# A two-layer diffusion backbone on one core: chunk rows two ahead, standing conv tiles, two-pass projections, another pace of modulation rows

## The chip, the core and the metric

The kernel runs on one core of a Trainium2 chip. A core has five engines, each with its own in-order queue: TensorE (PE in the profile, with its weight loads as PEld) for matmuls, VectorE (DVE), ScalarE (ACT) and GpSimd (POOL) for elementwise work, and SyncE (SP), which issues the DMAs here. [...] The metric is the device time of one execution in microseconds; the median over runs is compared.

## What is computed

Two post-norm layers over 512 latent tokens and 256 context tokens, width 1024, all in float32. Layer 0 mixes tokens by gated linear attention (GLA) with a low-rank decay, layer 1 by a bidirectional state-space scan (SSD). Each is followed by a squared-ReLU MLP of width 4096 (FFN), and each sub-layer is modulated by shift, scale and gate rows made from the conditioning vectors.

```python
m_l = jnp.split((s_lat @ ada_w[i] + ada_b[i])[:, None, :], 6, axis=-1)
ul = snake(modulate(hl, m_l[0], m_l[1]))
yc, yl = gla_mixer(...)  if kind == 0  else  ssd_mixer(...)
hl = layer_norm(ALPHA * hl + m_l[2] * snake(yl), ...)
hl = layer_norm(ALPHA * hl + m_l[5] * sq_relu_mlp(modulate(hl, m_l[3], m_l[4]), w1, w2), ...)
# GLA, the low-rank part: a is 2 x 16 columns of h @ w_in
logit = einsum('blzr,zrd->zbld', a.reshape(b, l, 2, 16), w_a2) + b_a2
# SSD: 32 heads of 64 in 8 groups, state 128
z, xbc, dt = jnp.split(h @ w_in, ...)
xbc = silu(dwconv(xbc, conv_w, conv_b))          # width 5
dt = softplus(dt + dt_bias)                       # 2 directions x 32 heads
# in a chunk: y = (c . b) * exp(cum_i - cum_j, masked) @ (x * dt), plus the carried state
```

## The kernel before

Activations lie with features on the 128 partitions and tokens along the row: 512 latent and 256 context columns. To keep float32 accuracy with fast matmuls, every operand is split into a high part and a low remainder (`xh`, `xl`; `wh`, `wl`; `rh`, `rl`), and `prod` (L240) runs three terms for each block of 128 features: high by high, low activations by high weights, high activations by low weights. So a 1024-wide projection of one 128-row output is 24 matmuls for each segment of columns. A weight tile is loaded into one of four `raw` buffers (L227), cast on ScalarE (`wh`, L203) and its remainder taken on VectorE (`wl`, L204); three of each are held.

The program is written as generators. The main line issues projections; `worked` counts the columns given to TensorE, in units of 768, and after each unit may advance a `side` generator (work of the previous stage) and, every `pace[0]` units, the `background` generator `ada_rows`. One step of the latter loads a 128x1024 block of modulation weights into a `raw` buffer and makes one or two multiply-and-sum passes over it on VectorE (L157). `mod(layer, m)` drains the background until the row it needs is there. The pace is 9 at first, 12 from the GLA layer on, and 21 in FFN 0, whose first block (`bi == 0`) begins with a pre-pass of `npre` units and ends with the gate row `mod(layer, 5)`. In the FFN, ScalarE makes `rr` and `rh`, GpSimd the square `rq` (L385) and VectorE the rest `rl` (L387).

The order in which the instructions stand in each engine's queue is not that of the program text: a scheduler lays them out ahead of time, and hands out the buffers of each ring (a tag with `bufs=n`) as it goes. A load into a ring buffer is issued when the last reader of the tile that held it has been scheduled.

GLA: `first_step` (L1143) runs four projections step by step while the layer's first modulation rows come in. The third of them (`j == 2`) is the low-rank one: the weights of 32 columns are repeated three times across the 96 output rows (`wsplit(..., 32, 3)`), so that rows 0 to 31, 32 to 63 and 64 to 95 of the result are the same; the last third is replaced by its remainder, so that `aT` holds high, high and low, against `a2`, which has `gla_a2` laid out to match.

SSD: first the step projection `dt` (64 columns of weights, `prod` with three terms), `dT`, six transposes (L802), softplus, cumulative sums by matmuls with triangles (`tri`, L821), and the rows `crow` and `crowc` written to DRAM, from where they are read back broadcast over partitions. Then eight groups g0 to g7, each with four convolutions `conv`: projection, copy into a padded tile `pre` (L857, L860), whose pad columns GpSimd clears each time (L855, L856, L859), five taps on VectorE in `cv` (L867), SiLU into `cf` (L869, L870). The rest of a group is the side generator `inner(g)`, which runs while the next group's projections go on: `heads_rows` (`ec`), `natural` (TensorE transposes L877 and ScalarE copies L878 into `Bn` and `xnat`), weighted x (`xw`, L931) and states (L943), `cbs` (the products of C and B, copied at L965), then for each of four chunks the decay masks.

A chunk's rows are two tiles of the ring `L` (`LB = 7` buffers), one per direction: a DMA broadcast from `crowc` (L910), a triangular select on GpSimd (L912), four exponentials on ScalarE with a per-head bias (L998, `decays`), their sum on GpSimd (L1001, `masks`), which frees the second tile, the product with `cbs` on VectorE, and the matmuls `outputs` (L1009), which free the first. The program asks for chunk 0's rows just before the inter-chunk part and for chunk c + 1's at the end of step c:

```python
Rs, Ms = {0: chunk_rows(0)}, {}
...
    if c + 1 < NLC:
        Rs[c + 1] = chunk_rows(c + 1)
```

## Time and profile before

| | us |
|---|---|
| runs | 1951.9, 1965.13, 1965.4 |
| median | 1965.13 |
| span of the profiled execution | 1959.6 |
| TensorE busy in it | 1881.3 |
| VectorE, ScalarE, GpSimd busy | 1254.9, 798.6, 410.8 |

Stages in the trace, by when TensorE works on them: GLA projections from 10 us, FFN 0 about 440 to 960, step projection and first SSD group to 1047, the groups g0 to g7 with their inner parts to about 1500, then the SSD output projection and FFN 1 to the end. In the lists of the profile a row reads: line, engine, operation, output tile <- input tiles, shape; in brackets the time that the engine stood idle before it and what ended the idle time. In the chain of waits each row is a piece of the path that ended last: start, length, what ran. A row of stretches gives length, then busy time of TensorE, weight loads, VectorE, ScalarE and GpSimd with their counts, the granted TensorE clock, the DMA share and GB/s.

### The profile page before, as it was taken

Reading aid. Unit: us, or ns where it says so; the run is one execution under the profiler, and the core shown is the slowest. Engines: PE = TensorE matmul, PEld = TensorE weight load, DVE = VectorE, ACT = ScalarE, POOL = GpSimd, SP = SyncE. Lnnn points to the kernel's source line nnn. Section 1 sums busy time; section 2 is a strip of 40 time slices with the busy share of each in tenths; the row PEclk is TensorE's granted clock in tenths of the full one; section 3 lists DMA queues with packets and bytes.
Section 4 is the critical chain, followed back from the end, with each engine's and each line's share of the span. In section 5 each row is a group of like instructions: output and inputs, shape, how many; then the busy total and the mean of one; then the engine's idle time right before and its main releaser. Section 6 shows DMA issues by size and latency. Waiting matters only on the chain.

```text
span 1959.6 us, 29026 instructions
## 1 busy us (share of the span) xinstructions
PE 1881.3 (96%) x11405; PEld 1604.9 (82%) x11405; DVE 1254.9 (64%) x1929; ACT 798.6 (41%) x1386; POOL 410.8 (21%) x448
## 2 busy tenths in 40 slices
PE   7999999999999999999999999999999999999997
PEld 5988888788788888888897787777877788888886
DVE  4798887888655444324578888777887673333345
ACT  3445456454113123122366555455543353323231
POOL 2134242202002002010104432333321321102012
PEclk9999999999999999999999999999999999999999
DMA  8423313214444444313134433333434523333331
GB/s 329 156 73 114 104 36 106 65 55 150 141 142 140 138 137 135 116 41 116 33 107 121 129 115 112 104 101 129 121 100 132 164 73 105 96 99 96 96 89 54
DMA packets 78936, 219.01 MB, mean 112 GB/s; under 512 B 11056, under 2 KB 15792, under 8 KB 78800
## 3 DMA queue, kind: packets, MB, share of 16 engines
q1 hardware_dynamic: 78800, 217.17, 35.1%
q8 instruction: 89, 1.46, 0.3%
q14 instruction: 47, 0.39, 0.1%
HBM read 209.01 MB, written 8.13 MB: 111 GB/s over the span
## 4 chain that ended last, share of the span: by engine, by line
PE 63%; DVE 13%; DMA 7%; ACT 6%; POOL 5%; issue 5%; SPq 0%; DVEq 0%; POOLq 0%; ACTq 0%
PE mm L240 54%; DMA L<-crowc 4%; POOL L L1001 1%; ACT L L998 1%; DMA raw<-in_ada_wr_dram 1%; DVE A L593 1%; PE sm L943 1%; DVE raw L157 1%; DVE cv L867 1%; POOL L L912 1%; PE sm L676 1%; DVE wl L204 1%; POOL W L612 1%; PE sm L986 1%; PE mm L520 1%
## 5 line engine op out<-in xcount | busy, mean ns | idle before, releaser
L240 PE MATMUL mm<-xh,wh 128*128 128x512 f32 (+1 forms) x1824 | 554.2, 357 | 2.8 <-ACT xh L1044 2.6
L240 PE MATMUL mm<-xl,wh 128*128 128x512 f32 (+1 forms) x1824 | 550.0, 354 | 1.5 <-DVE xl L1045 1.5
L240 PE MATMUL mm<-xh,wl 128*128 128x512 f32 (+1 forms) x1824 | 549.7, 353 | 1.4 <-DVE wl L204 1.4
L203 ACT CAST wh<-raw 128x1024 fp32r<-128x1024 f32 (+3 forms) x227 | 227.8, 1004 | 658.5 <-PE mm L240 617.3
L204 DVE TENSOR_TENSOR wl<-raw,wh 128x1024 fp32r<-128x1024 f32 (+3 forms) x227 | 275.6, 1215 | 173.6 <-ACT wh L203 170.1
L240 PEld LDWEIGHTS mm<-xh,wh 128*128 128x128 f32 x1824 | 304.4, 189 | 54.4 <-ACT xh L1044 3.8
L240 PEld LDWEIGHTS mm<-xl,wh 128*128 128x128 f32 x1824 | 303.7, 189 | 50.6 <-issue 3.1
L240 PEld LDWEIGHTS mm<-xh,wl 128*128 128x128 f32 x1824 | 303.5, 189 | 50.7 <-DVE wl L204 2.5
L385 POOL TENSOR_TENSOR rq<-rr 128x768 f32<-128x768 f32 (+1 forms) x62 | 104.6, 1687 | 684.7 <-ACT rr L384 648.4
L240 PE MATMUL mm<-rl,wh 128*128 128x512 f32 x704 | 212.5, 355 | 3.8 <-DVE rl L387 3.8
L240 PE MATMUL mm<-rh,wl 128*128 128x512 f32 x704 | 212.4, 355 | 0.0
L240 PE MATMUL mm<-rh,wh 128*128 128x512 f32 x704 | 212.1, 355 | 0.0
L419 DVE SCALAR_TENSOR_TENSOR acc<-mm,row,acc 128x256 f32<-128x256 f32 (+1 forms) x182 | 100.7, 580 | 150.4 <-PE mm L240 150.0
L157 DVE SCALAR_TENSOR_TENSOR raw<-raw,srow 128x1024 f32<-128x1024 f32 x104 | 131.6, 1268 | 83.0 <-DMA raw<-in_ada_wr_dram 81.8
L867 DVE SCALAR_TENSOR_TENSOR cv<-pre,cvec,cv 128x770 f32<-128x770 f32 (+1 forms) x128 | 135.2, 1057 | 14.9 <-ACT cv L865 11.9
L240 PEld LDWEIGHTS mm<-rl,wh 128*128 128x128 f32 x704 | 116.0, 189 | 23.8 <-DVE rl L387 4.2
L240 PEld LDWEIGHTS mm<-rh,wh 128*128 128x128 f32 x704 | 116.1, 189 | 19.6
L240 PEld LDWEIGHTS mm<-rh,wl 128*128 128x128 f32 x704 | 116.1, 189 | 19.6
L998 ACT ACTIVATE L<-L,lcol 128x128 f32<-128x128 f32 x256 | 81.9, 393 | 69.1 <-POOL L L912 69.1
L387 DVE TENSOR_TENSOR rl<-rq,rh 128x768 fp32r<-128x768 f32 (+2 forms) x67 | 53.2, 794 | 64.0 <-POOL rq L385 63.7
L912 POOL TENSOR_SCALAR_AFFINE_SELECT L<-L 128x512 f32<-128x512 f32 x64 | 52.2, 817 | 142.5 <-DMA L<-crowc 141.4
L869 ACT ACTIVATE cf<-cv 128x512 f32<-128x512 f32 (+1 forms) x56 | 27.6, 533 | 86.5 <-DVE cv L867 86.5
(290 smaller groups left out, 2513.0 us busy)
## 6 DMA issues: line engine op xcount, KB each, us to landing
raw<-in_ffn_w_dram SPq DMA_DIRECT2D x112, 512.0 KB, 3.8
raw<-in_ada_wr_dram SPq DMA_DIRECT2D x80, 512.0 KB, 3.7
raw<-in_ssd_w_in_dram SPq DMA_DIRECT2D x48, 512.0 KB, 3.9
L<-crowc SPq DMA_DIRECT2D x64, 256.0 KB, 3.8
raw<-in_ada_w_dram SPq DMA_DIRECT2D x16, 512.0 KB, 9.1
raw<-in_gla_w_in_dram SPq DMA_DIRECT2D x16, 512.0 KB, 3.7
ec<-crow SPq DMA_DIRECT2D x64, 128.0 KB, 3.0
acc<-in_xT_dram SPq DMA_DIRECT2D x14, 384.0 KB, 6.9
```

What stands on the lines that cost most here:

```text
L157: nc.vector.scalar_tensor_tensor(o, raw, 1.0, srow[s], ALU.mult, ALU.mult, accum_out=t[:, b, s:s + 1])
L203: nc.scalar.copy(h, src)
L204: nc.vector.tensor_sub(l, src, h.bitcast(F32))
L240: nc.tensor.matmul(part_of(ps, t0, n), a[:, k, :], b[:, t0:t0 + n], start=(k == 0 and i == 0), stop=(k == kt - 1 and i == 2))
L385: eng.tensor_mul(q[:, a:b], r[:, a:b], r[:, a:b])
L387: nc.vector.tensor_sub(rl[:, a:b], q[:, a:b], rh[:, a:b].bitcast(F32))
L419: nc.vector.scalar_tensor_tensor(acc[m][:, t0:t0 + n], part_of(ps, t0, n), gate[:, m, s:s + 1], (src or acc)[m][:, t0:t0 + n], ALU.mult, A ...
L520: nc.tensor.matmul(ps[:, 256 * tt:256 * tt + 256], a, b, start=(k == 0 and i == 0), stop=(k == KT - 1 and i == 2))
L867: nc.vector.scalar_tensor_tensor(c[:, 0:n], pre[:, t:t + n], cw(t), c[:, 0:n], ALU.mult, ALU.add)
L869: nc.scalar.activation(f[:, t0:t1], c[:, t0 + d:t1 + d], AF.Tanh)
L912: nc.gpsimd.affine_select(out=L[z], in_=L[z], compare_op=ALU.is_ge, fill=NEG, base=0, pattern=[[0, 4], [1 - 2 * z, P]], channel_multiplier ...
L998: nc.scalar.activation(t[:, h, :], t[:, h, :], AF.Exp, bias=lcol[:, c, r:r + 1])
```

## The change

Five things change; comment lines go as well, so that lines below move by up to 30.

```diff
-LB = 7
+LB = 10
@@ split products
+    def wstack(src, n):
+        ts = [wpool.tile([P, KT, P], F32R, tag=t, name=nm(t), bufs=3) for t in ("wh", "wl")]
+        r = P // n
+        for t in ts:
+            v = t[:, :, 0:P - n].rearrange("p k (r n) -> p k r n", n=n)
+            nc.scalar.copy(v, src.unsqueeze(2).to_broadcast([P, KT, r - 1, n]))
+        nc.vector.tensor_sub(ts[0][:, :, P - n:], src, ts[0][:, :, 0:n].bitcast(F32))
+        nc.gpsimd.memset(ts[1][:, :, P - n:].bitcast(F32), 0.0)
+        return ts
@@ ffn, bi == 0
                     f1(m, restsegs, held[m])
+                pace[0] = 11
...
                 gate = mod(layer, 5)
+                pace[0] = 22
@@ gla_layer
-        aT = gp.tile([96, NT], F32R, tag="aT", name="aT")
+        aT = gp.tile([P, NT], F32R, tag="aT", name="aT")
...
-        for r in range(0, 96, 32):
+        for r in range(0, P, 32):
@@ ssd_layer, step projection
-            w = wsplit(wload(ssd_w_dt), KT, 64)
+            w = wpool.tile([P, KT, P], F32R, tag="wh", name="wdt", bufs=3)
+            src = wload(ssd_w_dt)
+            split_to(w[:, :, 0:64], w[:, :, 64:], src)
+            def prod_dt(segs):
+                for k in range(KT):
+                    for i in range(2):
+                        for (t0, n, _) in segs:
+                            nc.tensor.matmul(part_of(ps, t0, n), w[:, k, :], xs[k][i][:, t0:t0 + n],
+                                             start=k + i == 0, stop=k + i == KT)
+                            worked(n)
-            prod(ps, w, xs, CTXL0, KT)
+            prod_dt(CTXL0)
...
-            nc.vector.tensor_tensor(v, pt, rowb[:, 0:64].unsqueeze(1).to_broadcast(sh), ALU.add)
+            for c0, c1 in ((0, 4), (4, 6)):
+                pt = sm_ps([P, 4, P])
+                for c in range(c0, c1):
+                    nc.tensor.transpose(pt[:, c - c0, :], dT[:, c * P:(c + 1) * P], ident)
+                vc, n = v[:, c0:c1], c1 - c0
+                nc.vector.tensor_tensor(vc, pt[:, 0:n, 0:64], rowb[...], ALU.add)
+                nc.vector.tensor_add(vc, vc, pt[:, 0:n, 64:])
@@ ssd_layer, conv
+        pres = [sp.tile([P, NT + 6], F32, tag="pre", name=nm("pre"), bufs=2) for _ in range(2)]
+        for t in pres:
+            for c in (0, 514, 772):
+                nc.gpsimd.memset(t[:, c:c + 2], 0.0)
...
-            pre = sp.tile([P, NT + 6], F32, tag="pre", name=nm("pre"), bufs=2)
+            pre = pres[0]
+            pres.reverse()
-            nc.gpsimd.memset(pre[:, 0:2], 0.0)
-            nc.gpsimd.memset(pre[:, 514:516], 0.0)
-                nc.gpsimd.memset(pre[:, 772:774], 0.0)
@@ inner
             Es = [heads_rows(i) for i in range(2)]
+            Rs, Ms = {c: chunk_rows(c) for c in range(2)}, {}
...
-            Rs, Ms = {0: chunk_rows(0)}, {}
...
-                if c + 1 < NLC:
-                    Rs[c + 1] = chunk_rows(c + 1)
+                if c + 2 < NLC:
+                    Rs[c + 2] = chunk_rows(c + 2)
@@ first_step
-                for i, (a, b) in enumerate(((w[0], xs[k][0]), (w[1], xs[k][0]), (w[0], xs[k][1]))):
+                terms = ((w[0], xs[k][0]), (w[1], xs[k][0]), (w[0], xs[k][1])) if j != 2 else zip(w, xs[k])
+                for i, (a, b) in enumerate(terms):
...
-                    ws.extend((wsplit(wload(gla_w_a), KT, 32, 3),
+                    ws.extend((wstack(wload(gla_w_a), 32),
@@ program
-    nc = _bacc.Bacc("TRN2", target_bir_lowering=False, num_devices=1)
+    nc = _bacc.Bacc("TRN2", target_bir_lowering=False, num_devices=1, dynamic_dma_scratch_size=1024)
```

The low-rank projection now has high, high, high, low weights in one tile and high, high, high, zero in the other: the first multiplies the high activations, the second the low ones, and the fourth block of 32 rows carries the high-by-low term into `aT` of 128 rows, to be summed by the product with `a2`. The step projection has high and low weights side by side in one 128-column tile, and the two halves are added after the transposes. The smaller scratch of the last line gives the room for the three more `L` buffers. The matmuls of TensorE go from 10436 to 10396: 16 fewer in `first_step`, 24 fewer in the step projection. GpSimd has 85 rows fewer.

How the rows stand on ScalarE at the end of g4's projections, where it copies the transposed tiles (L878), before:

```order
L203 CAST wh_12304<-raw_12302 128x1024
L878 COPY Bn_12069<-sm_12071 128x512
L878 COPY Bn_12069<-sm_12077 128x256
L878 COPY xnat_12070<-sm_12083 128x4x128
L878 COPY xnat_12070<-sm_12089 128x2x128
L998 ACTIVATE L_12904<-L_12904,lcol 128x128 x4
L878 COPY xnat_12070<-sm_12107 128x4x128
L878 COPY xnat_12070<-sm_12113 128x2x128
L998 ACTIVATE L_12957<-L_12957,lcol 128x128 x4
L965 COPY cbs_12167<-sm_12162 128x512
```

and after the change (L907 is L878 of before, L1028 is L998, L995 is L965):

```order
L203 CAST wh_12203<-raw_12201 128x1024
L907 COPY Bn_11985<-sm_11987 128x512
L907 COPY Bn_11985<-sm_11993 128x256
L907 COPY xnat_11986<-sm_11999 128x4x128
L907 COPY xnat_11986<-sm_12005 128x2x128
L1028 ACTIVATE L_13078<-L_13078,lcol 128x128 x4
L907 COPY xnat_11986<-sm_12023 128x4x128
L907 COPY xnat_11986<-sm_12029 128x2x128
L1028 ACTIVATE L_13087<-L_13087,lcol 128x128 x4
L995 COPY cbs_12083<-sm_12078 128x512
```

Nothing moved: two rows of exponentials stand among and behind the copies in both, on a tile further on in the count. The same holds for g2, g3 and g5.

The same place in g6, before:

```order
L203 CAST wh_13446<-raw_13444 128x1024
L878 COPY Bn_13211<-sm_13213 128x512
L878 COPY Bn_13211<-sm_13219 128x256
L878 COPY xnat_13212<-sm_13225 128x4x128
L878 COPY xnat_13212<-sm_13231 128x2x128
L998 ACTIVATE L_14084<-L_14084,lcol 128x128 x4
L878 COPY xnat_13212<-sm_13249 128x4x128
L878 COPY xnat_13212<-sm_13255 128x2x128
L998 ACTIVATE L_14136<-L_14136,lcol 128x128 x4
L965 COPY cbs_13309<-sm_13304 128x512
```

and after:

```order
L203 CAST wh_13315<-raw_13313 128x1024
L919 ACTIVATE zs_13013<-mm_13020 128x512
L907 COPY Bn_13097<-sm_13099 128x512
L907 COPY Bn_13097<-sm_13105 128x256
L907 COPY xnat_13098<-sm_13111 128x4x128
L907 COPY xnat_13098<-sm_13117 128x2x128
L907 COPY xnat_13098<-sm_13135 128x4x128
L907 COPY xnat_13098<-sm_13141 128x2x128
L995 COPY cbs_13195<-sm_13190 128x512
```

The two rows of exponentials are gone from it. Between the `cbs` copies of g5 and g6 there are 32 exponentials before and 20 after, between those of g6 and g7 twelve and none, and between those of g0 and g1 40 and 64. Of the latter, 26 stand in one row right behind `cbs` of g0, ahead of `cf` of the next convolution; the last two tiles among them are each loaded when the sum (L1031) of the pair before has freed a buffer. On SP, eight loads of `L` stand behind the `ec` rows of g0 ahead of the next weight load, where two stood.

VectorE's rows in the first block of FFN 0, from the first `rl` on, before (`junk` and `raw` are the two passes of a row step):

```order
L387 TENSOR_TENSOR rl_4682<-rq_4684,rh_4681 128x768
L204 TENSOR_TENSOR wl_4796<-raw_4793,wh_4795 128x1024
L387 TENSOR_TENSOR rl_4715<-rq_4717,rh_4714 128x768
L157 SCALAR_TENSOR_TENSOR raw_4819,row_4603<-raw_4819,srow_4598 128x1024
L387 TENSOR_TENSOR rl_4785<-rq_4787,rh_4784 128x768
L204 TENSOR_TENSOR wl_4866<-raw_4863,wh_4865 128x1024
L157 SCALAR_TENSOR_TENSOR junk_4885,row_4603<-raw_4883,srow_4597 128x1024
L204 TENSOR_TENSOR wl_4936<-raw_4933,wh_4935 128x1024
```

and after (L397 is L387 of before):

```order
L397 TENSOR_TENSOR rl_4668<-rq_4670,rh_4667 128x768
L157 SCALAR_TENSOR_TENSOR raw_4752,row_4589<-raw_4752,srow_4584 128x1024
L397 TENSOR_TENSOR rl_4701<-rq_4703,rh_4700 128x768
L204 TENSOR_TENSOR wl_4787<-raw_4784,wh_4786 128x1024
L397 TENSOR_TENSOR rl_4776<-rq_4778,rh_4775 128x768
L157 SCALAR_TENSOR_TENSOR junk_4798,row_4589<-raw_4796,srow_4583 128x1024
L157 SCALAR_TENSOR_TENSOR junk_4825,row_4589<-raw_4823,srow_4583 128x1024
L157 SCALAR_TENSOR_TENSOR raw_4796,row_4589<-raw_4796,srow_4584 128x1024
L157 SCALAR_TENSOR_TENSOR raw_4823,row_4589<-raw_4823,srow_4584 128x1024
L157 SCALAR_TENSOR_TENSOR junk_4852,row_4589<-raw_4850,srow_4583 128x1024
L204 TENSOR_TENSOR wl_4867<-raw_4864,wh_4866 128x1024
```

The first `wl` moved behind the second `rl`, and five passes stand between the third `rl` and the second `wl`, where none stood. Up to the last `rl` of this block there are 84 passes since the start, 75 before.

More of the change, by code (lines that the diff above doesn't have):

```diff
@@ L494, in gla_layer @@
             ps = part_of(first[2], t0, n)
-            nc.scalar.copy(aT[:, ts], ps[0:96])
+            nc.scalar.copy(aT[:, ts], ps)
             nc.vector.tensor_sub(aT[64:96, ts], ps[64:96], aT[64:96, ts].bitcast(F32))
@@ L794, in ssd_layer @@
                 nc.sync.dma_start(accd[k], acc0[k][:, :NL])
-            prod(ps, w, xs, L1, KT)
+            prod_dt(L1)
             prod(held[1], held[0], xs, L1, KT)
-            dT = tt([64, NT], "dT")
+            dT = tt([P, NT], "dT")
             for (t0, n, _) in BOTH:
-                nc.vector.tensor_copy(dT[:, t0:t0 + n], part_of(ps, t0, n)[0:64, :])
-            pt = sm_ps([P, NCH, 64])
-            for c in range(NCH):
-                nc.tensor.transpose(pt[:, c, :], dT[:, c * P:(c + 1) * P], ident[0:64, 0:64])
+                nc.vector.tensor_copy(dT[:, t0:t0 + n], part_of(ps, t0, n))
             sh = [P, NCH, 64]
@@ L1140, in first_step @@
                 w = ws[j]
[L1141 removed]
+                terms = ((w[0], xs[k][0]), (w[1], xs[k][0]), (w[0], xs[k][1])) if j != 2 else zip(w, xs[k])
+                for i, (a, b) in enumerate(terms):
                     for (t0, n, _) in segs:
                         nc.tensor.matmul(part_of(first[j], t0, n), a[:, k, :], b[:, t0:t0 + n],
[L1144 removed]
+                                         start=(k == 0 and i == 0), stop=(k == KT - 1 and i == (1 if j == 2 else 2)))
         m = ct([P, 2, 8, 2], "ada01")
```

6 lines of the change are left out of this document (3 added, 3 removed).

## The prediction

> **What bounds the kernel.** I read the page first, then the list of what TensorE waited for, then the timelines around the longest of those waits and the chain of waits there.
>
> ```profile
> span 1959.6 us, 29026 instructions
> PE 1881.3 (96%) x11405; PEld 1604.9 (82%) x11405; DVE 1254.9 (64%) x1929; ACT 798.6 (41%) x1386; POOL 410.8 (21%) x448
> ...
> PE sm L943 <- DVE xw L931: 15.4, 9, 3.6
> PE sm L877 <- ACT Bn L878: 7.5, 4, 2.9
> PE sm L125 <- DMA raw<-in_ada_w_dram: 5.7, 2, 5.2
> ...
> PE mm L240 <- DVE rl L387: 3.8, 1, 3.8
> ...
> PE sm L877 <- DVE cf L870: 3.3, 1, 3.3
> ```
>
> TensorE is busy for 1881.3 of 1959.6 us; only 78.3 us are idle. So there are two ways to gain: fewer matmuls, or fewer of these waits. The first two rows of the waits (15.4 + 7.5 = 22.9 us) are all in the SSD layer, once or twice in each of its eight head groups g0 to g7, where the transposed B and x tiles (`Bn`, `xnat`, L878) and the weighted x (`xw`, L931) come late. The row of 3.8 us is in the first FFN. A changed wait in any other place is worth little.
>
> All sums are against the profiled execution's 1959.6 us. The median of the runs shown is 1965.13 us, 5.5 us above that span, and the runs lie between 1951.9 and 1965.4; I subtract the sum from the median.
>
> **Low-rank projection of the GLA layer in two passes.** Eight k-steps lose one term of a 512-column and a 256-column matmul: 16 matmuls. Their cadence, from the timeline of TensorE (an "x2" row is two matmuls):
>
> ```profile
> 27.68 0.51 PE L1143 MATMUL mm<-xh,wl 128*128 128x512 f32 x2
> 28.03 0.53 PE L1143 MATMUL mm<-xl,wh 128*128 128x512 f32 x2
> 28.39 0.51 PE L1143 MATMUL mm<-xh,wh 128*128 128x512 f32 x2
> ...
> 25.00:59.00 34.00, 34.00 (x294) 27.28 (x293) 21.43 (x39) 12.89 (x22) 9.10 (x17) 1.00 0.69 258
> ```
>
> The rows start 0.35 us apart, one 512 and one 256 together. The window from 25 to 59 us (the columns behind the length are TensorE, weight load, VectorE, ScalarE, GpSimd) has TensorE busy throughout, so what is removed there counts in full: 8 x 0.35 = **-2.8 us**. Against it stand a wider cast on ScalarE ahead of the first use, two more `a2` loads on SP and 128 instead of 96 rows in the `aT` copies, which cost nothing more, since rows lie side by side. The cast is no larger than a weight cast (1.0 us below). I take 0 for these with 0 to +1 us as ends, since that stage waits for the `in_ada_w` loads at its start (5.7 us above) and not for ScalarE afterwards.
>
> **Step projection of the SSD layer in two passes.** It loses 24 matmuls of 256 columns, at the cadence of this stage:
>
> ```profile
> 1005.55 0.28 PE L240 MATMUL mm<-xl,wh 128*128 128x256 f32 x1
> 1005.67 0.28 PE L240 MATMUL mm<-xh,wl 128*128 128x256 f32 x1
> 1005.79 0.28 PE L240 MATMUL mm<-xh,wh 128*128 128x256 f32 x1
> ...
> 1013.52 0.89 PE L821 MATMUL sm<-dv,tri 128*128 128x192 f32 x4 [0.88 <-DVE dv L816]
> ```
>
> 24 x 0.12 = **-2.9 us**. The chain behind it gets longer: six transposes into two tiles instead of one, and four adds on VectorE instead of one. It already ends last once: TensorE waits 0.88 us for `dv`. In the changed order more matmuls stand ahead of that row. Ends 0 and +2 us (three more adds, each below the 0.5 to 1.0 us that VectorE's rows of 512 to 770 columns show); I take **+0.5 us**, near the lower end, as work was moved in.
>
> **Chunk rows two ahead, ten buffers.** This is the part whose size is open. The last long stall of the SSD layer, in g6, read backwards in the chain of waits:
>
> ```profile
> 1415.46 1.32 POOL L L1001
> ...
> 1416.80 4.50 DMA L<-crowc
> ...
> 1421.43 0.65 POOL L L912
> ...
> 1422.10 1.28 ACT L L998 x4
> 1423.37 0.74 ACT xnat L878 x2
> ...
> 1424.14 1.26 DVE xw L931 x2
> ...
> 1425.54 1.95 PE sm L943 x4
> ...
> 1416.96 0.85 ACT L878 COPY xnat<-sm 128x512 f32<-128x512 f32 x2
> ```
>
> The mask add (L1001) frees a buffer of the ring `L`; the next load of chunk rows takes 4.50 us, its select 0.65; four exponentials (L998) of that same tile stand on ScalarE between the two pairs of `xnat` copies, so these copies, `xw` and TensorE wait for the load, although they do not need it. More buffers would cure that only if the exponentials behind a just-freed buffer moved away from the copies. The order shown with the change says they do not: from g2 to g5 ScalarE, GpSimd and SP have the same rows in the same places, with tiles three further on, and each load still waits for the mask add just ahead of it. The scheduler had run the loads ahead until the ring was full, and it does so again with a ring of ten. So I cost the stalls of g1 to g5 at no change. In g6 the loads have run out three tiles earlier: no exponentials stand among the copies, and g6's wait goes: **-3.6 us** (the longest in the first row of waits). What is late next there is `xw` itself: the first pair of copies ran at 1416.96 (last row, from ScalarE's timeline), so without the load the second pair ends at about 1418.5 and `xw` at 1419.8, before TensorE stopped (1425.5 - 3.6 = 1421.9). I count the full 3.6; ends 0 and -3.6.
>
> The 24 exponentials (six tiles of four) that leave g6 and g7, twelve from each, now stand between the `cbs` copies of g0 and g1, at 0.32 us each 7.7 us of ScalarE:
>
> ```profile
> 1066.32 0.58 ACT L965 COPY cbs<-sm 128x512 f32<-128x512 f32 x1 [3.15 <-PE sm L963]
> 1068.09 1.28 ACT L998 ACTIVATE L<-L,lcol 128x128 f32<-128x128 f32 x4 [1.19 <-POOL L L912]
> 1072.44 1.06 ACT L203 CAST wh<-raw 128x1024 fp32r<-128x1024 f32 x1 [3.08 <-PE mm L240]
> ...
> 1078.02 0.94 ACT L869 ACTIVATE cf<-cv 128x512 f32<-128x512 f32 x2 [1.28 <-DVE cv L867]
> ...
> 1085.07 1.03 ACT L203 CAST wh<-raw 128x1024 fp32r<-128x1024 f32 x1
> ...
> 1090.00:1150.00 60.00, 55.83 (x317) 45.25 (x316) 53.61 (x76) 34.30 (x74) 22.10 (x28) 1.00 0.40 123
> ```
>
> ScalarE is busy 34.3 of 60 us there, so it has room on the whole. But behind `cbs` of g0 some 25 exponentials now stand in a row ahead of `cf` (L869), and their last two tiles go round the loop of the chain above twice: 2 x (1.32 + 4.50 + 0.65 + 1.28) = 15.5 us after 1067, so `cf` comes at about 1083 instead of 1078. The next weight cast and the next `pre` copy stand behind it, and came at 1085 anyway: the lateness is taken up before TensorE sees it. I take 0. Ends: +6 us (the 5 us reach TensorE, and 1 more at the next conv) and -3 us (the stall of 3.3 us at g0 for `cf`, which fewer GpSimd rows could shorten). On SP eight L loads instead of two stand ahead of a weight load, 6 x 0.33 us of issue; that weight's cast comes over 15 us later.
>
> ```profile
> L910 SPq DMA_DIRECT2D L<-crowc x64: 319/326/1569, 1023.6 to 1457.5; - x64
> 1390.87 0.10 POOL L855 MEMSET pre<- 128x2 f32 x1 [6.66 <-DVE cv L867]
> ```
>
> **Standing conv tiles.** Some 85 memsets of 0.10 us or less go from GpSimd, which is 21% busy. In the chain above GpSimd waits for a DMA, not for a memset: 0, ends -2 and 0 us.
>
> **Pace of the modulation rows.** It matters in the first block of FFN 0 alone. There VectorE makes `wl` (L204) and `rl` (L387) for TensorE, and a row step is two passes (L157) of 1.15 us each from start to start (the first two rows):
>
> ```profile
> 455.12 1.21 DVE L157 SCALAR_TENSOR_TENSOR junk<-raw,srow 128x1024 f32<-128x1024 f32 x1
> ...
> 456.27 1.21 DVE L157 SCALAR_TENSOR_TENSOR raw<-raw,srow 128x1024 f32<-128x1024 f32 x1
> ...
> 458.85 0.96 DVE L387 TENSOR_TENSOR rl<-rq,rh 128x768 fp32r<-128x768 f32 x1 [1.35 <-POOL rq L385]
> 459.72 1.22 DVE L204 TENSOR_TENSOR wl<-raw,wh 128x1024 fp32r<-128x1024 f32 x1
> 462.30 0.96 DVE L387 TENSOR_TENSOR rl<-rq,rh 128x768 fp32r<-128x768 f32 x1 [1.36 <-POOL rq L385]
> ...
> 465.75 0.96 DVE L387 TENSOR_TENSOR rl<-rq,rh 128x768 fp32r<-128x768 f32 x1 [1.35 <-POOL rq L385]
> ...
> 510.34 1.22 DVE L157 SCALAR_TENSOR_TENSOR junk<-raw,srow 128x1024 f32<-128x1024 f32 x1 [3.70 <-DMA raw<-in_ada_wr_dram]
> ...
> 513.63 1.01 PE L240 MATMUL mm<-rl,wh 128*128 128x512 f32 x2 [3.83 <-DVE rl L387]
> ```
>
> The wait of 3.83 us is there because the rows are late at the end of the block: VectorE stands in a row step whose load has not landed (3.70 us) ahead of `rl`. With 11 the rows finish earlier and this wait goes: -3.8. But in the changed order the first `wl` stands behind the second `rl`, which cannot start before 462.30: `wl` ends at 462.30 + 0.87 + 1.15 = 464.3 instead of 459.72 + 1.15 = 460.9. TensorE used it at once: +3.4. The second `wl` stands behind five passes more: the third `rl` ends at 465.75 + 0.87 = 466.6, five passes at 472.4, `wl` at 473.5. TensorE wants it one unit of 24 such pairs as above, 24 x 0.35 = 8.4 us, after 464.3, at 472.7: +0.8. Sum **+0.4 us**, ends -3.8 (both new waits hidden) and +4.2 (the old wait stays as a third).
>
> **Sum:** -2.8 - 2.9 + 0.5 - 3.6 + 0.4 = -8.4 us, which gives 1965.1 - 8.4 = 1956.7, say **1957 us**, 0.4% less.
>
> **Rivals.**
> *All SSD stalls go.* The loop (add, load, select, exponentials) is what the stalls wait for, and three more buffers are three tiles of slack. If the loads then land ahead of the copies, the other 22.9 - 3.6 = 19.3 us go as well: 1937.4 us. [...] The trace speaks for it so far that the load starts 0.02 us after the add; the unchanged order of g2 to g5 speaks against it.
> *The pace starves TensorE, slower than before.* In the changed order 84 passes stand ahead of the block's last `rl` and 75 before: 4.5 row steps more, through the same four `raw` buffers as the weights. If each brings the uncovered 3.70 us of the row at 510.34 and the waits above stay, that is 4.5 x 3.7 + 4.2 = 20.9 us in place of 0.4: 1977.2 us. It is slower than before from two such waits on (8.8 us of gains elsewhere against 4.2 + 2 x 3.7), and by over 1% only if a step brings 5.4 us. For it: VectorE waits for these loads in the profile. Against it: the loads are asked for earlier, and a unit of 8.4 us holds two row steps, one `wl` and one `rl` (4.6 + 1.15 + 0.9).
> *The look-ahead does nothing at all.* If in g6 another operand is late in the place of the load, only matmuls are gained: 1956.7 + 3.6 = 1960.3 us; with the 6 us at g0 and g1 it is 1966.3, no change.
>
> One more weighing, on the stall of 3.6 us in g6:
>
> ```profile
> 1394.00:1455.00 61.00, 57.24 (x329) 46.30 (x328) 49.24 (x74) 32.96 (x72) 20.92 (x28) 1.00 0.37 118
> ```
>
> The granted clock (the 1.00) does not drop around it, so I add nothing. [...]
>
> **How the numbers follow.** The forecast as summed has 0.45, within 1949 to 1964 by its ends. The look-ahead without effect has 0.2, all SSD stalls gone 0.2, the starving pace 0.15. A difference under about 1% (19.7 us) can hardly be told from no change here. Faster by over 1% is below 1945.5: most of the first rival, 0.18. Slower by over 1% is above 1984.8: a starving pace with longer waits than priced, 0.06. The rest, 0.76, is within 1%. The range of 1940 to 1972 leaves out the lower half of the first rival and the upper half of the starving pace.
>
> **What would show it.** Right: TensorE's count falls by 40; the waits for `xw` keep about 12 us in g1 to g5 and lose the one in g6; the wait for `rl` in FFN 0 is gone and one for `wl` of about 3 us stands at the start of the fourth unit of its first block. Wrong: the rows for `xw` and `Bn` fall to a few us (the look-ahead works in every group), or FFN 0's first block takes longer than before, or a wait of several us for `cf` appears between 1070 and 1115 us.

## The result and the profile after

| | before | after |
|---|---|---|
| median of 8 runs, us | 1958.3 | 1978.55 |
| runs, from and to (after: seven of the eight) | 1951.9 to 1965.4 | 1972.94 to 1984.5 |
| after : before | | 1.0105 [1.0074, 1.0137] |
| span of the profiled execution | 1959.6 | 1971.2 |

The changed kernel is slower by about 1%, where 0.4% less was forecast. One of its eight runs took 3081.61 us at a granted clock of 0.557, against 0.983 to 0.986 in the seven others, and is left out of the ratio. The profiled execution of the changed kernel ran 1972.94 us, the fastest of its runs, and the median without the run of 3081.61 is 1977.03; the profiled execution of the kernel before lies some 3 us above its median. So the two traces are only 11.6 us apart, and what follows explains these 11.6 us, not the whole of the timed difference.

The page of the changed kernel, its first lines and its list of what TensorE waited for (total us, number of waits, longest):

```profile
span 1971.2 us, 28815 instructions
...
PE 1882.0 (95%) x11365; PEld 1607.1 (82%) x11365; DVE 1260.5 (64%) x1932; ACT 801.5 (41%) x1387; POOL 414.6 (21%) x363
```

```profile
PE sm L973 <- DVE xw L961: 14.6, 6, 3.5
PE sm L1039 <- issue: 8.6, 1, 8.6
PE sm L586 <- DVE E L616: 8.3, 10, 3.3
PE mm L250 <- DVE wl L204: 8.3, 5, 3.6
...
PE mm L250 <- DVE rl L397: 4.0, 1, 4.0
PE sm L906 <- DVE cf L899: 3.9, 1, 3.9
...
PE sm L906 <- ACT Bn L907: 2.5, 2, 1.7
```

TensorE has 40 matmuls fewer (11405 to 11365) and is busy 0.7 us longer (1881.3 to 1882.0). The waits of the SSD layer for `xw` add up to about the old sum (15.4 before), and those for `Bn` are smaller (7.5 before). New are one wait of 8.6 us, larger ones for `E` (5.3 before, in the GLA layer) and for `wl` (1.4 before), while the wait for `rl`, which was to go, is still there (3.8 before).

To see where the time went, the start of one matmul at the end of each stage was read from both traces. The stages: the end of `first_step` (the low-rank projection lies in it, at 58.7 us before); the end of the GLA layer's attention (399.9); the start of FFN 0's second products (949.6, which takes in what lies between); the step projection's first triangle (1013.5); the `cbs` products of g0 (1065.2) and of g1 (1122.3); and the end. Between these marks TensorE runs the same number of matmuls in every kernel, apart from those that the change removes, with two exceptions: with the new step projection 14 matmuls of 512 columns more stand ahead of the first triangle than with the old one, and 28 fewer between it and the `cbs` of g0. At 0.35 - 0.12 = 0.23 us each (in float32, without the split, a product of 512 columns takes 0.9 us: two of L943 in 1.8 us from 1425.54 us before), the 14 move some 3.2 us of work ahead of the triangle; the sum of the two stages up to the `cbs` of g1 is not touched by that. The first line of the table below says how much longer the changed kernel took for each stage. The loss lies in three places: the GLA layer behind the low-rank projection (+7.7), FFN 0 (+3.2), and the stretch from the first triangle to the `cbs` of g1 (+12.6).

### The profile page after: what moved, and what is told of

It reads as the page before. It is cut to its first block, busy times and chain, and to the rows that moved or that the text cites. A ratio compares the mean times of both kernels' runs of the same rounds, so it can differ in the third digit from the quotient of the medians.

```text
span 1971.2 us, 28815 instructions
## 1 busy us (share of the span) xinstructions
PE 1882.0 (95%) x11365; PEld 1607.1 (82%) x11365; DVE 1260.5 (64%) x1932; ACT 801.5 (41%) x1387; POOL 414.6 (21%) x363
## 4 chain that ended last, share of the span: by engine, by line
PE 63%; DVE 15%; ACT 6%; issue 5%; DMA 5%; POOL 5%; SPq 0%; DVEq 0%; POOLq 0%; ACTq 0%
PE mm L250 54%; DMA L<-crowc 3%; DVE cv L896 2%; POOL L L1031 1%; DVE A L605 1%; PE sm L973 1%; DVE wl L204 1%; PE sm L688 1%; DVE E L616 1%; DVE raw L157 1%; PE mm L532 1%; ACT xn L325 1%; ACT wh L203 1%; ACT L L1028 1%; DVE lnst L315 1%
## 5 line engine op out<-in xcount | busy, mean ns | idle before, releaser
L250 PEld LDWEIGHTS mm<-rl,wh 128*128 128x128 f32 x704 | 116.3, 189 | 23.3 <-DVE rl L397 4.3
L1028 ACT ACTIVATE L<-L,lcol 128x128 f32<-128x128 f32 x256 | 81.7, 392 | 64.9 <-POOL L L941 64.9
L397 DVE TENSOR_TENSOR rl<-rq,rh 128x768 fp32r<-128x768 f32 (+2 forms) x67 | 53.2, 795 | 70.7 <-POOL rq L395 69.1
L941 POOL TENSOR_SCALAR_AFFINE_SELECT L<-L 128x512 f32<-128x512 f32 x64 | 57.2, 898 | 167.3 <-DMA L<-crowc 165.4
```

The lines of the kernel that those rows point to most:

```text
L250: nc.tensor.matmul(part_of(ps, t0, n), a[:, k, :], b[:, t0:t0 + n], start=(k == 0 and i == 0), stop=(k == kt - 1 and i == 2))
L397: nc.vector.tensor_sub(rl[:, a:b], q[:, a:b], rh[:, a:b].bitcast(F32))
L941: nc.gpsimd.affine_select(out=L[z], in_=L[z], compare_op=ALU.is_ge, fill=NEG, base=0, pattern=[[0, 4], [1 - 2 * z, P]], channel_multiplier ...
L1028: nc.scalar.activation(t[:, h, :], t[:, h, :], AF.Exp, bias=lcol[:, c, r:r + 1])
```

## The experiments

Each of the kernels below was profiled, and its stages were read the same way. All numbers are us longer than in the trace of the kernel before; the last columns are the median of its runs (and how many), and the ratio to the kernel before where there are several.

| kernel | to the end of `first_step` | rest of GLA | FFN 0 | first triangle | to `cbs` of g1 | g1 to the end | sum | median (runs) | ratio |
|---|---|---|---|---|---|---|---|---|---|
| the change | -1.8 | +7.7 | +3.2 | -0.8 | +12.6 | -9.3 | +11.6 | 1978.55 (8) | 1.0105 [1.0074, 1.0137] |
| x1 chunk rows undone | -1.9 | +7.4 | +2.6 | -0.8 | +4.7 | -3.1 | +8.9 | 1976.85 (10) | 1.0097 [1.0067, 1.0127] |
| x2 low-rank undone | +0.1 | -0.5 | +4.8 | -0.7 | +13.3 | -8.9 | +8.1 | 1978.67 (5) | 1.0116 [1.0054, 1.0178] |
| x3 pace undone | -1.9 | +7.2 | -0.6 | -0.8 | +11.9 | -6.5 | +9.3 | 1974.03 (9) | 1.0088 [1.0057, 1.0118] |
| x4 `T` on VectorE | -1.3 | +10.9 | +2.7 | -0.8 | +12.9 | -18.6 | +5.8 | 1967.69 (10) | 1.0048 [1.0020, 1.0076] |
| y2 ring of 7, two ahead | -1.3 | +8.2 | +10.9 | -0.8 | +8.6 | -6.2 | +19.4 | 1980.7 (1) | |
| y4 x1 and pads undone | -1.6 | +7.7 | +2.9 | -0.8 | +5.6 | -3.1 | +10.7 | 1972.03 (1) | |
| ring of 8 | -1.0 | +8.1 | +3.1 | -0.7 | +11.5 | -6.6 | +14.4 | 1975.79 (1) | |
| ring of 13 | -1.4 | +8.9 | +10.9 | -0.8 | +14.9 | -9.2 | +23.3 | 1984.6 (1) | |
| z2 x1 and step projection undone | -1.3 | +9.0 | +4.9 | -1.1 | -1.4 | -6.9 | +3.2 | 1964.54 (1) | |
| z3 before, 16 matmuls fewer | -1.9 | +6.9 | +1.0 | -1.1 | +0.5 | -8.9 | -3.5 | 1957.8 (1) | |
| y3 before, `T` on VectorE | -0.1 | -0.8 | +0.6 | -0.2 | -1.2 | -11.7 | -13.4 | 1953.29 (10) | 0.9976 [0.9953, 0.9999] |
| y3 with a ring of 8 | +0.5 | -0.6 | +7.5 | -0.1 | 0.0 | -15.1 | -7.8 | 1954.37 (10) | 0.9981 [0.9956, 1.0007] |

How far such a number can be trusted shows in two columns. "Rest of GLA" is +6.9 or more in all ten kernels whose low-rank projection has 16 matmuls fewer, and -0.8 to -0.5 in the three others: that is a step of the kernel. "g1 to the end" is -8.9 in z3, whose SSD code is that of before and whose rows there stand in the same order: the same order can differ by 9 us between two executions in that stretch. So nothing below rests on that column as a whole. Of its parts, only the step to the `cbs` of g6 falls into two groups: -3.7 to -4.9 us in the five kernels with ten or more buffers, -0.4 to -2.6 in the eight with seven or eight.

### The chunk rows undone

```diff
-LB = 10
+LB = 7
-            Rs, Ms = {c: chunk_rows(c) for c in range(2)}, {}
+            Rs, Ms = {0: chunk_rows(0)}, {}
-                if c + 2 < NLC:
-                    Rs[c + 2] = chunk_rows(c + 2)
+                if c + 1 < NLC:
+                    Rs[c + 1] = chunk_rows(c + 1)
```

> The changed kernel with seven L buffers and the chunk rows asked for one ahead, where they were. Theory (queue): the 8.6 us stall of TensorE in g0 comes from GpSimd's queue, where the add of T stands behind four rounds of load, select and sum; with the old rows in place it is gone, g1 to g6 have their old stalls back, and the span falls by about 5 us (from the first triangle matmul to the end of the SSD layer the changed kernel lost 13.2 - 8.2 = 5.0 us). Rival (the step projection's longer chain is what makes g0 late): the stall in g0 stays above 5 us and the span falls by under 2 us.

To `cbs` of g1 the loss fell from 12.6 to 4.7 us; the span fell by 2.7 us of the 5 that were expected, and the two ratios can't be told apart. So by these two traces 7.9 us of that stretch go with the chunk rows, and 4.7 stay without them. These are differences of totals, not one stall each: up to the `cbs` of g0 the changed kernel is 6.7 us shorter than x1, with the same matmuls, and from there to g1 it is 14.6 us longer. How this loss comes about stands on ScalarE, in the timeline of the changed kernel between the `cbs` copy of g0 and the next `cf` (start, length, operation, count, wait ahead of it):

```profile
1069.17 0.59 ACT L995 COPY cbs<-sm 128x512 f32<-128x512 f32 x1 [0.54 <-PE sm L993]
1069.66 2.15 ACT L1028 ACTIVATE L<-L,lcol 128x128 f32<-128x128 f32 x7
1075.33 1.28 ACT L1028 ACTIVATE L<-L,lcol 128x128 f32<-128x128 f32 x4 [3.52 <-POOL L L941]
1080.74 1.28 ACT L1028 ACTIVATE L<-L,lcol 128x128 f32<-128x128 f32 x4 [4.13 <-POOL L L941]
1086.68 1.28 ACT L1028 ACTIVATE L<-L,lcol 128x128 f32<-128x128 f32 x4 [4.66 <-POOL L L941]
1090.02 1.28 ACT L1028 ACTIVATE L<-L,lcol 128x128 f32<-128x128 f32 x4 [2.06 <-POOL L L941]
1093.44 0.99 ACT L1028 ACTIVATE L<-L,lcol 128x128 f32<-128x128 f32 x3 [2.14 <-POOL L L941]
1094.34 0.92 ACT L898 ACTIVATE cf<-cv 128x512 f32<-128x512 f32 x2
```

26 exponentials stand there in a row, as the prediction had counted (some 25). But they go round the loop of add, load, select and exponentials five times, not twice: five waits for the select (L941), 16.5 us together. `cf` comes 25.2 us behind the `cbs` copy; before it was 11.7 (1066.32 to 1078.02). VectorE and TensorE at the same place:

```profile
1094.68 0.75 DVE L1019 SCALAR_TENSOR_TENSOR T<-cf,dcol,T 128x512 f32<-128x512 f32 x1 [13.02 <-POOL T L1018]
```

```profile
1089.16 0.51 PE L250 MATMUL mm<-xl,wh 128*128 128x512 f32 x2
1098.27 1.12 PE L1039 MATMUL sm<-L,xnat 128*64 128x128 f32 x8 [8.60 <-issue]
...
1100.13 0.84 PE L250 MATMUL mm<-xh,wh 128*128 128x512 f32 x2
1100.77 0.84 PE L250 MATMUL mm<-xl,wh 128*128 128x512 f32 x2
```

TensorE stops for 8.6 us. The page names nothing that ended this wait ("issue"), but the matmul reads `L`, and the product that makes it stands on VectorE behind the rows that wait for `T` and `cf`, and ends 0.1 us before the matmul starts:

```profile
1097.48 0.68 DVE L1032 TENSOR_TENSOR L<-L,cbs 128x512 f32<-128x512 f32 x1
```

Afterwards the rows start 0.64 us apart instead of 0.35 (1100.13 to 1100.77).

### `T` taken off GpSimd

VectorE's 13.0 us are put down to an add of `T` (L1018) on GpSimd, which stands there behind the selects of the same loop. Two causes for the 8.6 us were then open: GpSimd's queue (the add), or ScalarE's (`cf`).

```diff
-                nc.gpsimd.tensor_add(T[:, i], T[:, i], E)
+                nc.vector.tensor_add(T[:, i], T[:, i], E)
```

> The changed kernel with the add into T (two per group) on VectorE in place of GpSimd; everything else as changed. Theory (queue): in g0 VectorE no longer waits 13 us for GpSimd's add behind the loop of loads; the 8.6 us stall of TensorE falls below 3 us and the span by 4 to 9 us, less up to 2 us for 16 more adds of 0.7 us on VectorE. Rival (the exponentials in a row on ScalarE are what delays g0, through cf): the stall moves to the first tap or cf of g1 and stays above 6 us, and the span falls by under 2 us.

The stretch stayed at +12.9, and TensorE's stall grew, so GpSimd's queue alone is not the cause. VectorE's row and its wait, now with the add on VectorE, and TensorE's stall:

```profile
1096.50 1.03 DVE L899 SCALAR_TENSOR_TENSOR cf<-cf,cv 128x512 f32<-128x512 f32 x2 [9.27 <-ACT cf L898]
...
1104.06 1.12 PE L1039 MATMUL sm<-L,xnat 128*64 128x128 f32 x8 [12.14 <-issue]
```

It now waits 9.27 us for the `cf` of ScalarE, in the same place. Both queues stand behind the loop of chunk rows; with one freed the other holds. So the rival was right about the place. Its other half, a span that falls by under 2 us, was not: the kernel is faster than the changed one (1.0048 against 1.0105, intervals that just overlap). In the trace the gain lies from g3 on, and how the add costs time there was not looked into.

### Ring or placement, and how large a ring

Two ahead with seven buffers, and the changed kernel with 13 and with 8 buffers:

```diff
-LB = 10
+LB = 7      (y2; then 13, and 8)
```

> The changed kernel with seven L buffers, chunk rows still asked for two ahead at the new place. Theory (the ring alone moves the work; the scheduler runs the loads ahead until the buffers are out, wherever they are asked for): the steps of the SSD layer are those of the kernel with both undone, +1.3 us from the triangles to cbs of g0 and +3.4 us from there to g1 against the kernel before, and the 8.6 us stall is gone. Rival (asking two ahead is what crowds g0): the step from g0 to g1 stays above +10 us.

> The changed kernel with thirteen L buffers. Theory (each buffer puts eight more exponentials behind cbs of g0, which go round the loop of sum, load, select at some 5.5 us a tile pair, ahead of cf): the step from cbs of g0 to g1 grows from +18 us (ten buffers; +3.4 with seven) by about 4.9 us a buffer to +30 to +36 us against the kernel before, and g5 and g6 win 3 to 5 us each. Rival (three more buffers were too few): the stall at g0 shrinks and the step falls below +12 us.

> The changed kernel with eight L buffers. Fourteen exponentials stand in a row ahead of cf in g0, eight with seven buffers, 26 with ten, 35 with thirteen (steps from cbs of g0 to g1: +3.4, +18.0, +20.6 us). If the length of that row is what costs, the step is +6 to +11 us here. If it is a threshold (a second round of the loop that catches GpSimd's and VectorE's queues), it stays near +3.4 or is already above +14.

| buffers (changed kernel) | 7, one ahead | 7, two ahead | 8 | 10 | 13 |
|---|---|---|---|---|---|
| first triangle to `cbs` of g1 | +4.7 | +8.6 | +11.5 | +12.6 | +14.9 |
| of it up to `cbs` of g0 | +1.3 | +1.7 | +1.8 | -5.4 | -5.7 |
| from there to `cbs` of g1 | +3.4 | +6.9 | +9.7 | +18.0 | +20.6 |
| exponentials between `cbs` of g0 and `cf` | 8 | 8 | 14 | 26 | 35 |

The two rows that part at the `cbs` of g0 can be compared across these five kernels, which run the same matmuls in each; against the kernel before, matmuls have moved over the `cbs` of g0.

Asking two chunks ahead leaves the rows of TensorE, VectorE and ScalarE in the order of x1 (on GpSimd one select stands elsewhere), and yet it has +8.6 against +4.7, in one execution each: so differences of some 4 us in this stretch say little. The size of the ring sets the order. From `cbs` of g0 to that of g1 the loss grows with the number of exponentials. With eight buffers it came to +9.7 us, inside the +6 to +11 that were expected if the length of the row is the price; with 13 it came to +20.6 and not to the +30 to +36 expected. There 19 of the 35 exponentials are ready, and four rounds wait, 9.7 us in all against the 16.5 above. What more buffers lose behind `cbs` of g0 they win back in part ahead of it: the changed kernel's `cf` there waits 0.84 us for VectorE, where that of x1 stands behind an exponential that waits 4.72 us for a chunk row (below). So the sum grows less, and between 8, 10 and 13 buffers it can't be ranked.

### The step projection undone as well

x1 kept +4.7 in this stretch. ScalarE in x1 in g0, one copy earlier:

```profile
1057.43 3.05 ACT L1027 ACTIVATE L<-L,lcol 128x128 f32<-128x128 f32 x10
1065.20 0.40 ACT L1027 ACTIVATE L<-L,lcol 128x128 f32<-128x128 f32 x1 [4.72 <-POOL L L941]
1065.51 0.92 ACT L898 ACTIVATE cf<-cv 128x512 f32<-128x512 f32 x2
```

Here too an exponential that waits 4.72 us for a chunk row stands ahead of `cf`. Either the standing pads or the step projection could have moved it; y4 clears the pads each time as before, z2 has the step projection of before (three terms, six transposes, one add), both on top of x1.

```diff
-            pre = pres[0]
-            pres.reverse()
+            pre = sp.tile([P, NT + 6], F32, tag="pre", name=nm("pre"), bufs=2)
+            nc.gpsimd.memset(pre[:, 0:2], 0.0)
+            nc.gpsimd.memset(pre[:, 514:516], 0.0)
...
```

> The changed kernel with the chunk rows and ring as before and the conv pads cleared each time again; low-rank, step projection and pace as changed. If the standing pads are what cost the remaining 1.3 + 3.4 us up to g1, both steps come back to within 1 us of the kernel before. Rival (the step projection with its longer chain): they stay, at +3 us or more together.

```diff
-            prod_dt(CTXL0)
+            prod(ps, w, xs, CTXL0, KT)
...
```

> The changed kernel with chunk rows, ring and step projection as before; pads, low-rank and pace as changed. The steps from the triangles to cbs of g0 and on to g1 were +1.3 and +3.4 us with the chunk rows undone, and stayed with the pads undone too. If the step projection's longer chain costs them, both fall to within 1 us of the kernel before, and the -0.8 us up to the triangles goes to about 0. Rival (a shift of the whole, by which loads or background work come at another point): they stay at +3 us or more.

With the pads undone the stretch stays at +5.6; with the step projection undone it is -1.4. So the pads cost nothing that shows, and the step projection does. Taken over both columns, so that the mark at the triangle drops out, x1 is 3.9 us longer than the kernel before and z2 2.5 us shorter: two terms in place of three cost 6.4 us up to the `cbs` of g1, where the 24 matmuls less were to save 2.9. The stage up to the triangle alone can't show that saving, since the 14 matmuls that moved into it make up for the 24 that went: it is 0.7 to 0.8 us shorter than before with two terms, and 0.1 to 1.1 us shorter with three. The expectation that it would go back to 0 in z2 failed (-1.1). What in the new step projection changes the order was not told apart: fewer matmuls for the scheduler, one weight tile in place of two, two transposed tiles and four adds, or the counter `worked`, which is given 24 x 256 columns, eight units, less and so advances the other generators later.

With the step projection of before, eight buffers and `T` on VectorE, this stretch costs 0.0, where the changed kernel with eight has +11.5; `T` on VectorE is no cure by itself (x4 in the table). So the ring's price seems to hang on the new order too, but that kernel differs in the other parts of the change as well, and ten buffers with the old step projection were not tried.

### The low-rank projection undone, and alone

```diff
-                    ws.extend((wstack(wload(gla_w_a), 32),
+                    ws.extend((wsplit(wload(gla_w_a), KT, 32, 3),
...
```

> The changed kernel with the low-rank projection in three passes and 96 rows again. Theory (order): the two passes save 1.8 us up to 57 us, but the order of the rest of the GLA layer comes out another way and loses 7.7 us between 57 and 400 us; undone, TensorE reaches the output projection of the GLA layer 5.9 us earlier and the span falls by 5 to 7 us. Rival (the loss in the GLA layer comes from elsewhere, a slower clock or slower loads in that execution): the layer still ends some 6 us later than in the kernel before, and the span falls by nothing or rises by 2 us.

Undone, the loss in the GLA layer is gone (-0.5), and the early gain with it (+0.1). The sum fell by 3.5 us only and the median by nothing, as FFN 0 and the stretch to g1 came out higher; the effect is shown in the trace, not in the run times. TensorE in the changed kernel, behind the two-pass projection, and then the row of the window from 134 to 140 us:

```profile
130.44 1.09 PE L586 MATMUL sm<-E 128*64 128x64 f32 x24 [3.28 <-DVE E L616]
133.86 1.01 PE L250 MATMUL mm<-xh,wl 128*128 128x512 f32 x2 [2.33 <-DVE wl L204]
134.67 0.84 PE L250 MATMUL mm<-xh,wh 128*128 128x512 f32 x2
...
137.87 0.52 PE L250 MATMUL mm<-xh,wl 128*128 128x512 f32 x2
138.22 0.51 PE L250 MATMUL mm<-xh,wh 128*128 128x512 f32 x2
```

```profile
134.00:140.00 6.00, 6.00 (x25) 5.15 (x26) 5.90 (x6) 0.00 (x0) 0.00 (x0) 0.68 0.30 87
```

Two waits in a row, 3.28 and 2.33 us, then six rows 0.64 us or more apart (133.86 to 137.87) and a granted clock of 0.68 in the window. VectorE is busy 5.90 of these 6 us. What moved is the `wl` of the next projection. VectorE and TensorE before, and VectorE after the change:

```profile
123.43 1.23 DVE L204 TENSOR_TENSOR wl<-raw,wh 128x1024 fp32r<-128x1024 f32 x1
...
130.35 2.39 DVE L604 TENSOR_TENSOR E<-E,qk 128x1536 f32<-128x1536 f32 x1
...
132.79 0.92 PE L574 MATMUL sm<-E 128*64 128x64 f32 x24 [1.73 <-DVE E L604]
```

```profile
128.54 1.84 DVE L616 TENSOR_TENSOR E<-E,qk 128x1536 f32<-128x1536 f32 x1
...
132.58 1.23 DVE L204 TENSOR_TENSOR wl<-raw,wh 128x1024 fp32r<-128x1024 f32 x1
```

Before, this `wl` stands ahead of the last two `E` rows, and TensorE runs eight rows of that projection before it needs `E`. After, it stands behind the last `E`: TensorE has only two rows to run, waits for `E`, and then for `wl`. The rival to "fewer matmuls change the order" was that the new weight tile or the wider `aT` does it. z3 is the kernel before with the third term of the low-rank projection left out (low activations by high weights are not computed), nothing else:

```diff
-                for i, (a, b) in enumerate(((w[0], xs[k][0]), (w[1], xs[k][0]), (w[0], xs[k][1]))):
+                for i, (a, b) in enumerate(((w[0], xs[k][0]), (w[1], xs[k][0]), (w[0], xs[k][1]))[:2 if j == 2 else 3]):
...
-                                         start=(k == 0 and i == 0), stop=(k == KT - 1 and i == 2))
+                                         start=(k == 0 and i == 0), stop=(k == KT - 1 and i == (1 if j == 2 else 2)))
```

> The kernel before, but the low-rank projection leaves out its third term (low activations by high weights): 16 matmuls fewer, nothing else; 96 rows, the same tiles and casts. Theory (order: the scheduler sees the stage 2.8 us shorter and lays the rest of the GLA layer out another way): the first 57 us get 2 to 3 us shorter, and the stretch from there to the output projection 6 to 9 us longer, so the span is 4 to 6 us longer with 16 matmuls less. Rival (the 128-row tiles or the casts of the change cost it): the span is 2 to 3 us shorter.

TensorE in z3:

```profile
130.16 1.55 PE L574 MATMUL sm<-E 128*64 128x64 f32 x24 [3.27 <-DVE E L604]
...
133.58 1.01 PE L240 MATMUL mm<-xh,wl 128*128 128x512 f32 x2 [1.88 <-DVE wl L204]
134.39 0.84 PE L240 MATMUL mm<-xh,wh 128*128 128x512 f32 x2
```

16 matmuls fewer are enough: -1.9 us at once, then +6.9, with the same two waits, and in both kernels a third of 2.34 us for `on` at 168 us (0.32 before). The span of z3 came out 3.5 us shorter, not 4 to 6 longer: by that number alone the rival would have won. But 8.9 us of it come from the stretch from g1 to the end, where the rows stand as before, and the two stages that the theory named came out as it said. In z3 and in the changed kernel the rows of VectorE from here to the end of the layer stand in the same order, and those of ScalarE but for one copy; it is not the order of before. `first_step` does not feed the counter `worked`, so the program asks for the rest in the same order as before, and only the scheduler can have moved it. That it does so because it reckons with a shorter stage is argued, not shown; that the 16 matmuls do it is shown.

### The pace undone

```diff
-                pace[0] = 11
-                pace[0] = 22
```

> The changed kernel with the pace left at 21 in the FFN of layer 0. Theory: the stall for wl (3.6 us at 466 us) goes, the one for rl stays at about 3.8 us, and the first block is 3 to 4 us shorter; the span falls by as much. Rival (the modulation rows cost the same wherever they stand): the stall for rl grows by what the one for wl loses, and the span stays within 1 us.

FFN 0 fell from +3.2 to -0.6, so by these two traces the pace costs about 3.8 us. The others bear it out: leaving out three slower executions (last section), that column is +2.6 to +4.9 in the seven kernels with the new pace and -0.6 to +1.0 in the three with the old one. The wait for `wl` that the prediction had named came, on TensorE, and is followed by slow rows:

```profile
469.39 1.01 PE L250 MATMUL mm<-xh,wl 128*128 128x512 f32 x2 [3.63 <-DVE wl L204]
470.20 0.84 PE L250 MATMUL mm<-xh,wh 128*128 128x512 f32 x2
470.84 0.84 PE L250 MATMUL mm<-xl,wh 128*128 128x512 f32 x2
```

In x3 no wait for `wl` is over 1.9 us, and that longest one (1.87 us) stands in the GLA layer, at 133.70 us. The wait for `rl` at the end of the block stayed, at 4.0 us (3.9 in x3). VectorE ahead of it:

```profile
518.63 1.73 DVE L157 SCALAR_TENSOR_TENSOR junk<-raw,srow 128x1024 f32<-128x1024 f32 x1 [0.95 <-DMA raw<-in_ada_wr_dram]
...
520.29 1.21 DVE L204 TENSOR_TENSOR wl<-raw,wh 128x1024 fp32r<-128x1024 f32 x1
521.42 1.21 DVE L157 SCALAR_TENSOR_TENSOR raw<-raw,srow 128x1024 f32<-128x1024 f32 x1
...
522.57 0.95 DVE L397 TENSOR_TENSOR rl<-rq,rh 128x768 fp32r<-128x768 f32 x1
```

The load is late by 0.95 us instead of 3.70, but a `wl` and two passes stand between it and `rl`, where it was a `wl` and one pass.

### Two versions of the kernel before

x4's gain from g3 on suggested the same one line on the kernel before (y3), and, to see what a ring of eight does with the old step projection, that with `LB = 8`.

> The kernel before with the add into T on VectorE in place of GpSimd, nothing else. In the changed kernel this took 4.3, 4.3, 3.2, 4.6 and 2.0 us from the groups g3 to g7. If GpSimd's add of T delays the loads of the next chunk rows in every group, it does the same here: 8 to 15 us less, so about 1945 to 1950 us. Rival (the gain there came from the ten buffers): within 3 us of the kernel before.

> The kernel before with the add into T on VectorE and eight L buffers. By the first theory the eighth buffer costs 3 to 5 us at g0 and wins about 3 us at the end, so it is within 3 us of the same kernel with seven buffers (0.998 of before). If the add's move has freed GpSimd's queue enough, it is faster than that by over 3 us.

The first is 0.24% faster than the kernel before, by an interval that ends at 0.9999: its median is 3.8 us lower, neither the 8 to 15 of the expectation nor within the 3 of its rival. The second can't be told from the kernel before, and is within 1.1 us of the first, as expected. The larger ring adds nothing here either.

## Why the prediction was wrong

Its steps against the trace:

| step | predicted | measured |
|---|---|---|
| low-rank projection, in its own stage | -2.8 (with 0 to +1 for casts) | -1.8 |
| what follows in the GLA layer | nothing costed | +7.7 |
| step projection, in its own stage | -2.9 + 0.5 | -0.8, with 14 matmuls moved in |
| the same, two stages on (g0 and g1) | nothing costed | +4.7 in x1 |
| 24 more exponentials at g0 and g1 | 0, ends -3 and +6 | +7.9 against x1 |
| g1 to g5 | `xw` keeps about 12 us | 14.6 us for `xw`, six waits |
| g6 | -3.6 | -3.9 |
| pace in FFN 0 | -3.8 + 3.4 + 0.8 = +0.4 | +3.2 |
| pads | 0 | nothing seen |

The gains counted for the low-rank matmuls and for g6 are there, the first in part; the one for the pace is not, and the larger losses come from rows that the sum did not cost. Two remarks on its numbers: the base of 1965.1 is the median of three runs, that of eight is 1958.3; and its own ends, added up, reach from -18.1 to +7.5 us, 1947 to 1973, not "1949 to 1964".

**What held.** The order of g1 to g5 is the one that the prediction read from the change, the waits for `xw` stand, and g6 gains what was said: its wait for `xw` is gone. The `aT` copies cost nothing more with 128 rows: 576 and 370 ns with 96 (L495), 582 and 372 ns with 128 (L507). The rival in which all SSD stalls go fell: the `Bn` waits are 5.0 us smaller, but in z3 and y3, with seven buffers, they are smaller too (5.6 and 0.3 against 7.5), and what g0 and g1 lose is more. The sign of being wrong that it gave, "a wait of several us for `cf`" between 1070 and 1115 us, came in kind: the 8.60 us at 1098, for a product that stands behind `cf`.

**The exponentials at g0 and g1.** The step that failed is "their last two tiles go round the loop of the chain above twice", "so `cf` comes at about 1083 instead of 1078", and "the lateness is taken up before TensorE sees it". The place was right and the size wrong: five rounds, `cf` at 1094.3, and a stall of 8.6 us. The prediction took all tiles but the last two for ready; in the trace 7 of the 26 exponentials are, and each further group waits. The end of +6 us was too near: it counted one delayed engine, while VectorE's queue, through `T` and `cf`, hung on the loop in two ways.

**The rest of GLA.** No step of the sum was for it: "what is removed there counts in full", and the end of +1 us was for casts. A window with a busy TensorE shows what a removed matmul saves there; it does not show what the shortened stage does to the rows behind, and z3 shows that this was the larger part, by +6.9 against -1.9. The same holds of the step projection: its matmuls went, but by another order up to g1 it cost 6.4 us (x1 against z2) where -2.4 was forecast.

**The pace.** Of the two new waits for `wl` the first came as forecast (3.63 us from 465.8, for +3.4); the second, +0.8, does not show. What failed is "With 11 the rows finish earlier and this wait goes: -3.8". It is the end that the prediction had given, "+4.2 (the old wait stays as a third)". It named the load of 3.70 us as the cause, and that did shrink to 0.95; the work in VectorE's queue behind it, one pass longer than before, was what was late next, and it had not been counted.

**The clock.** "so I add nothing" was read from a window of 61 us around g6 with 1.00. For g6 it was right; for the other stalls, the old one at `rl` and the new ones, the sum has no such term and needed one. Windows of 5 us, of the kernel before at its `rl` stall and at g6, and of the changed one at g0:

```profile
513.00:518.00 5.00, 4.37 (x13) 3.76 (x14) 3.41 (x6) 1.04 (x1) 0.00 (x0) 0.50 0.69 193
1425.00:1430.00 5.00, 4.46 (x21) 3.32 (x22) 5.00 (x15) 1.09 (x4) 0.63 (x1) 1.00 0.14 52
```

```profile
1098.00:1103.00 5.00, 4.73 (x19) 3.95 (x20) 5.00 (x6) 1.22 (x2) 2.98 (x2) 0.50 0.36 122
```

The granted clock is 0.50 in the first and the last window, and 1.00 at g6. In the GLA rows above, the step to the next row is 0.81 us once and 0.64 five times instead of 0.35: 0.46 + 5 x 0.29 = 1.9 us more behind the stalls of 3.28 and 2.33 us. The length of a stall alone does not tell: the clock was 0.68 behind those two, with matmuls between them (134 to 140 us), 0.66 behind the 3.63 us in FFN 0 of the changed kernel (469 to 474 us), and 1.00 behind the 3.64 us at g6. What sets it the traces don't show.

**The size of the ring.** The ground of the first rival, that three more buffers are three tiles of slack for the loop, is borne out in g6 only. From g1 to g5 the waits for `xw` stayed, 14.6 us with ten buffers and 13.8 with thirteen (15.4 before, g6 with it), and g0 and g1 cost more with the larger rings, in one execution each.

**What stays open.** The causes sum to 5.9 (GLA) + 3.2 + 12.6 - 0.8 = 20.9 us up to the `cbs` of g1, and 9.3 us come back behind it, 3.9 of them in g6. How much of the other 5.4 the ring gives and how much is one execution against another can't be told, since z3 gets 8.9 us there with the old order. The parts were told apart by their stages in single traces; in run times only x4 (just) and the two last versions (clearly) stand below the changed kernel among those with several runs. Undoing one part did not give its share back in the median (1976.85, 1978.67 and 1974.03).

## What to carry to other kernels

Where a scheduler lays out the queues, a removed matmul is worth its own time only if the rows behind it keep their places: print the order for the next stages too, and look on each queue for a row that waits for a DMA and now stands ahead of a row that TensorE needs. A stretch between two marks can be compared only if the same work stands between them: count the matmuls. A ring that is always filled was not made looser by more buffers in g1 to g5; they let more waiting rows stand ahead of other work at its start, and helped in g6, where the loads had run out. Behind the stalls of 3.28 and 2.33 us in the GLA layer the slow matmuls cost 1.9 us more; look at the granted clock in a window of a few us there (0.68 in 6 us), and not at that of a long stretch alone.

## What was not expected of the hardware

A stretch of FFN 0 in which TensorE never stops took another time in different executions at the same granted clock. Windows from 530 to 640 us, of the changed kernel and of y2:

```profile
530.00:640.00 110.00, 110.00 (x637) 97.00 (x636) 56.41 (x81) 23.37 (x31) 11.20 (x6) 1.00 0.48 147
```

```profile
530.00:640.00 110.00, 110.00 (x624) 95.36 (x624) 56.53 (x81) 23.36 (x31) 10.32 (x6) 1.00 0.46 141
```

637 matmuls in 110 us against 624: 172.7 against 176.3 ns each, at 1.00 in both. Three of the 14 profiled executions (y2, the ring of 13, and y3 with a ring of 8) have 624 or 625 matmuls in this window, the other eleven 631 to 637; the three stand some 6 to 8 us higher in the FFN 0 column than their likes. y2 and x1 have the same order of rows on TensorE, VectorE and ScalarE, and 624 and 636 matmuls in the window; so it seems to go with the execution and not with the code, and would then be a part of the spread of the runs. Each kernel has only one trace. What sets it the traces don't show.
